# S5 states with real and imaginary part of one group on the 128 partitions, and one row load of the S5 time steps, in a hybrid encoder trunk

## The chip, the cores and the metric

The kernel runs on one core of a Trainium2 chip. The metric is the device time of one execution in microseconds (us). Times stand as the median of several runs. One further execution is taken by the hardware profiler; all rows below come from it.

## The reference

One residual layer over 2048 tokens of width 1024, in float32. The normalised input goes through one projection into twelve 512-wide pieces and a gate. Four branches (S5, retention, differential attention, memory attention) read the pieces; their outputs are gated, projected, merged and put through an output projection. The change touches the S5 branch alone: 32 groups of 16 channels, each with a diagonal complex state of 64 numbers.

```python
def s5_branch(u, lam_re, lam_im, log_dt, b_re, b_im, c_re, c_im, d_skip, w_glu, b_glu):
    ...
    dt = jnp.exp(log_dt.astype(f32))[:, None]
    mag = jnp.exp(lr * dt)
    ab_re = mag * jnp.cos(li * dt)
    ab_im = mag * jnp.sin(li * dt)
    ...
    bu_re = jnp.einsum('bsgh,gph->bsgp', ug, bb_re)
    bu_im = jnp.einsum('bsgh,gph->bsgp', ug, bb_im)
    ...
    _, _, xr, xi = lax.associative_scan(_ssm_combine, (a_re, a_im, bu_re, bu_im), axis=1)
    y = (jnp.einsum('bsgp,ghp->bsgh', xr, c_re.astype(f32))
         - jnp.einsum('bsgp,ghp->bsgh', xi, c_im.astype(f32)))
    y = y.reshape(bsz, seq, BRANCH_W) + d_skip.astype(f32) * u32
    z = jax.nn.gelu(y)
```

## The kernel before, in words

The sequence is worked in two blocks of 1024 tokens. In each block the stages follow one another: retention, differential attention, the other input projections, then memory attention, merge and output. Large matrix products are made of three passes over split operands (a high part and a rest, names ending in h and l): a weight tile `w_r` is loaded by SP (a DMA queue), ScalarE (ACT) rounds it to `w5h`, and VectorE (DVE) or GpSimd (POOL) makes the rest `w5l` (line 443). At the start the tiles of x are loaded (`n_x`, line 557), scaled by a root mean square whose power is taken on POOL (line 138), turned by TensorE (PE, line 574) and split into `xh` and `xl`; then the first product of retention can begin (lines 74 to 76). `w_r` has four buffers, so the fifth weight load waits until the first tile is split.

The order of the work is written as events with due times; a scheduler below the program then sets the order of each engine's instructions. Each engine runs its own list strictly in order.

S5 runs eight steps of time as one: 128 steps of a scan per block. Its matrices are made once, in `setup_s5`, beside the retention of the first block: four passes over four pairs of groups each, which write to a scratch tensor in HBM, `mats_d`, 1280 columns for each of 16 pairs. Each pass makes a table of cosines and sines (`tab`), the input matrices (`gm`, turned and stored as `ev`), the output matrices (`ca`) and a direct term (`tpad`). `tab` and `gm` share one buffer. The time steps `log_dt` come by two DMAs on ACT's queue (line 1593), element by element, with groups 2j on partitions 0 to 63 and groups 2j+1 on 64 to 127, before the first weights are asked for; POOL takes their exponential (`dt`, line 194).

The scan itself is done beside the input projections of each block: `s5_scan`, once for each of 16 pairs, in steps between the products of the projections (line 1332). Both groups of a pair stand on the partitions, 64 states each, and the free dimension holds real part and imaginary part:

```python
        for g2 in range(2):
            r0 = g2 * 64
            for i in range(2):
                PE.matmul(v[r0:r0 + 64, i * 128:(i + 1) * 128], fm[:, i, r0:r0 + 64], u[:, g2, :], start=True, stop=True)
```

So four products with 64 columns of weights go in. DVE turns the result by the table (lines 998 to 1003), scans (line 1007), turns back (lines 1010 to 1016). For the way out each group takes one product of the direct term and two of the state (real and imaginary), whose weights are zero on the other group's 64 partitions (lines 1021 and 1023); the zeros are stored at setup (line 404). A float32 product of 128 columns shows as two records in the trace.

Of the kernel before, what the change touches and what calls it, by code (L numbers as in the profile page):

```python
# [11 lines left out]
F32 = mybir.dt.float32  # L12
# [3 lines left out]
ALU = mybir.AluOpType  # L16
# [12 lines left out]
NPAIR = 16  # L29
# [7 lines left out]
def bc(ap, pos, n):  # L37
    dims = [list(e) for e in ap.ap]
    dims.insert(pos, [0, n])
    return bass.AP(ap.tensor, ap.offset, dims)  # L40
# [3 lines left out]
def trunk_kernel(ctx, tc, a):  # L44
    nc = tc.nc
    V, A, G, PE, DMA = nc.vector, nc.scalar, nc.gpsimd, nc.tensor, nc.sync
# [10 lines left out]
    const = ctx.enter_context(pool("const"))  # L57
# [56 lines left out]
    rho = const.tile([128, NPAIR], F32, name="rho")  # L114
    ldt = const.tile([128, NPAIR], F32, name="ldt")
    carry = const.tile([128, 2, NPAIR], F32, name="carry")
# [5 lines left out]
    mats_d = dram.tile([128, NPAIR, 1280], F32, name="mats_d")  # L122
# [19 lines left out]
    def setup_vectors(p):  # L142
# [3 lines left out]
        r0 = 0  # L146
        for nm, n in rows:
            src = a[nm]
# [4 lines left out]
        pt = ps_tr()  # L153
# [7 lines left out]
        V.tensor_scalar(HEAD_G, HEAD_G, 0.5 * (1.0 - LAMBDA_INIT), None, op0=ALU.mult)  # L161
        lt = p.tile([128, 4, 64], F32, name="lt")
# [12 lines left out]
    def setup_s5(p):  # L175
# [5 lines left out]
        def tt(o, x, y, op, eng=V):  # L181
            eng.tensor_tensor(o, x, y, op=op)
# [16 lines left out]
        t0, t1 = small("t0"), small("t1")  # L199
# [12 lines left out]
        c1 = 6.28125  # L212
# [53 lines left out]
        tt(rho, t0, t0, ALU.mult)  # L266
# [29 lines left out]
        zero = p.tile([128, 128], F32, name="zero")  # L296
        V.memset(zero, 0.0)
        dsk = p.tile([32, 16], F32, name="dsk")
        DMA.dma_start(out=dsk, in_=a["ssm_d"][0].rearrange("(g h) -> g h", h=16))
        pt = ps_tr()  # L300
# [3 lines left out]
        m = 4  # L304
        for j0 in range(0, n, m):
# [23 lines left out]
            DMA.dma_start(out=mats_d[:, js, 1024:1280], in_=tab.rearrange("p j r c -> p j (r c)"))  # L329
# [27 lines left out]
            for j in range(0, m, 2):  # L357
                pt = ps_tr()
                for q in range(4):
                    PE.transpose(pt[:, q * 128:(q + 1) * 128],  # L360
                                 gm[:, q % 2, j + q // 2].rearrange("p s h -> p (s h)"), ident)
                ev = p.tile([128, 2, 256], F32, name="ev", bufs=1)
                A.copy(ev.rearrange("p a b -> p (a b)"), pt)
                DMA.dma_start(out=mats_d[:, j0 + j:j0 + j + 2, 0:256], in_=ev)
                yield
# [32 lines left out]
            for g2 in range(2):  # L398
                r0, r1 = g2 * 64, 64 - g2 * 64
                for i in range(2):  # L400
                    c0 = 256 + (g2 * 2 + i) * 128
                    DMA.dma_start(out=mats_d[r0:r0 + 64, js, c0:c0 + 128],
                                  in_=ca[r0:r0 + 64, i, :, 1:9, :].rearrange("p j s h -> p j (s h)"))
                    DMA.dma_start(out=mats_d[r1:r1 + 64, js, c0:c0 + 128], in_=bc(zero[r1:r1 + 64], 1, m))
                yield
# [17 lines left out]
            for s in range(8):  # L423
                for g2 in range(2):
                    DMA.dma_start(out=mats_d[s * 16:(s + 1) * 16, js, 768 + g2 * 128:896 + g2 * 128],
                                  in_=tpad[:, :, g2, 128 - 16 * s:256 - 16 * s])
                if s % 4 == 3:
                    yield
# [558 lines left out]
    def s5_scan(b, j, p, u, mt):  # L987
        fm, em0, em1, dm, tb = [mt[:, i, :].rearrange("p (r c) -> p r c", r=2) for i in range(5)]
        v = ps_o()
        for g2 in range(2):  # L990
            r0 = g2 * 64
            for i in range(2):
                PE.matmul(v[r0:r0 + 64, i * 128:(i + 1) * 128], fm[:, i, r0:r0 + 64], u[:, g2, :], start=True, stop=True)
        v2 = v[:, 0:256].rearrange("p (r c) -> p r c", r=2)
        cosb, sinb = bc(tb[:, 0, :], 1, 2), bc(tb[:, 1, :], 1, 2)
        p1 = p.tile([128, 2, 128], F32, name="s_p1", tag="s_p1", bufs=1)
        p2 = p.tile([128, 2, 128], F32, name="s_p2", tag="s_p2", bufs=1)
        V.tensor_tensor(p1, v2, cosb, op=ALU.mult)
        V.tensor_tensor(p2, v2, sinb, op=ALU.mult)
        yield  # L1000
        w = p.tile([128, 2, 128], F32, name="s_w", bufs=1)
        V.tensor_tensor(w[:, 0, :], p1[:, 0, :], p2[:, 1, :], op=ALU.add)
        V.tensor_tensor(w[:, 1, :], p1[:, 1, :], p2[:, 0, :], op=ALU.subtract)
        y = p.tile([128, 2, 128], F32, name="s_y", bufs=1)
        rb = rho[:, j:j + 1].to_broadcast([128, 128])
        for i in range(2):
            V.tensor_tensor_scan(y[:, i, :], rb, w[:, i, :], carry[:, i, j:j + 1], op0=ALU.mult, op1=ALU.add)
        q1 = p.tile([128, 2, 128], F32, name="s_q1", tag="s_p1", bufs=1)
        q2 = p.tile([128, 2, 128], F32, name="s_q2", tag="s_p2", bufs=1)
        V.tensor_tensor(q1, y, cosb, op=ALU.mult)  # L1010
        V.tensor_tensor(q2, y, sinb, op=ALU.mult)
# [3 lines left out]
        V.tensor_tensor(x[:, 0, 1:129], q1[:, 0, :], q2[:, 1, :], op=ALU.subtract)  # L1015
        V.tensor_tensor(x[:, 1, 1:129], q2[:, 0, :], q1[:, 1, :], op=ALU.add)
        V.tensor_copy(carry[:, :, j], x[:, :, 128])
        yield
        for g2 in range(2):
            out = v[:, 256 + g2 * 128:384 + g2 * 128]  # L1020
            PE.matmul(out, dm[:, g2, :], u[:, g2, :], start=True, stop=False)
            for i in range(2):
                PE.matmul(out, (em0, em1)[g2][:, i, :], x[:, i, 0:128], start=False, stop=i == 1)
# [555 lines left out]
    for b in range(NBLK):  # L1579
# [4 lines left out]
        if b == 0:  # L1584
            with ExitStack() as sx:
# [5 lines left out]
                for g2 in range(2):  # L1591
                    src = a["ssm_log_dt"]
                    A.dma_start(out=ldt[g2 * 64:(g2 + 1) * 64, :],
                                in_=bass.AP(src.tensor, src.offset + g2, [[0, 64], [2, NPAIR]]))
# [107 lines left out]
```

## Time and profile before

| what | value |
|---|---|
| three runs, median (lowest to highest) | 3048.71 us (3043.44 to 3057.92) |
| the profiled execution, its own time | 3045.78 us |
| its span, first to last instruction | 3043.5 us |
| PE busy | 2899.1 us, 95% |
| PE weight loads busy | 2381.9 us, 78% |
| DVE / ACT / POOL busy | 1920.5 / 1332.3 / 1247.0 us |
| mean granted TensorE clock | 0.990 |
| DMA, mean over the span | 116 GB/s |

A row of the view by windows gives, for a stretch of the span, its length, then the busy time and the count of instructions of PE, of PE's weight loads, of DVE, ACT and POOL, then the granted clock, the DMA engines' busy share and GB/s. A row of the timeline gives start, duration, engine, line, operation, tiles and count; in brackets stands how long the engine sat idle before it, and what ended that. SPq and ACTq are DMA issues.

### The profile page before, as it was taken

To read this page: it belongs to the slowest core of one execution; us is meant where nothing else is said; L and a number is where in the kernel's file an instruction comes from. 1 tells how busy PE (TensorE), PEld (TensorE's weight loads), DVE (VectorE), ACT (ScalarE), POOL (GpSimd) and SP (SyncE) were. 2 spreads that over 40 slices of the span, in tenths; PEclk is the share of its full clock that TensorE was granted. 3 is DMA by queue.
4 is the path that set the end of the run, shared out by engine and by line. 5 is a ranking of instruction groups with operands and counts; after the bars stand their busy time and mean duration, and the time that the engine had idled before them with its cause. 6 is when DMAs were issued, how large, how long until landed. Compare 5 with 4: busy or idle time off the path is not lost. (4 is left out here: it accounts for less than half of the span.)

```text
span 3043.5 us, 43500 instructions
## 1 busy us (share of the span) xinstructions
PE 2899.1 (95%) x14514; PEld 2381.9 (78%) x14514; DVE 1920.5 (63%) x4613; ACT 1332.3 (44%) x3357; POOL 1247.0 (41%) x1157
## 2 busy tenths in 40 slices
PE   5999999998999999999999999999999999999999
PEld 4777877777888888777788878878878888887777
DVE  5885587766655545656544378888766555446654
ACT  3323355563333344423433257767733333444332
POOL 2543533334444442555132242232244444434560
PEclk9999999999999999999999999999999999999999
DMA  5332422233444436555521220120134444355653
GB/s 154 97 92 77 126 68 68 68 97 119 141 150 142 134 109 204 188 182 175 161 69 43 63 66 22 58 61 21 59 115 142 144 142 137 125 184 166 194 167 96
DMA packets 319341, 351.75 MB, mean 116 GB/s; under 512 B 28479, under 2 KB 238478, under 8 KB 319118
## 3 DMA queue, kind: packets, MB, share of 16 engines
q1 hardware_dynamic: 314734, 340.59, 35.7%
q0 software_dynamic: 2304, 8.39, 0.9%
q8 instruction: 114, 1.87, 0.3%
q14 instruction: 109, 0.89, 0.1%
q10 hardware_dynamic: 2080, 0.01, 0.0%
HBM read 247.98 MB, written 100.93 MB: 115 GB/s over the span
## 5 line engine op out<-in xcount | busy, mean ns | idle before, releaser
L1294 POOL TENSOR_TENSOR p_l<-p_r,p_h 128x512 fp32r<-128x512 f32 x260 | 368.4, 1420 | 458.3 <-ACT p_h L1293 445.3
L74 PE MATMUL mm<-w5h,xh 128*128 128x512 f32 x1024 | 436.3, 426 | 17.9 <-ACT xh L577 16.5
L75 PE MATMUL mm<-w5l,xh 128*128 128x512 f32 x1024 | 406.7, 397 | 3.5 <-POOL w5l L443 3.5
L76 PE MATMUL mm<-w5h,xl 128*128 128x512 f32 x1024 | 406.9, 397 | 0.0
L138 POOL TENSOR_TENSOR rms_r<-rms_m,mhalf 128x1 f32<-128x1 f32 (+1 forms) x228 | 179.0, 787 | 488.2 <-DVE rms_m L136 422.6
L1293 ACT CAST p_h<-p_r 128x512 fp32r<-128x512 f32 x260 | 160.3, 621 | 376.6 <-PE mm L1332 85.8
L758 ACT ACTIVATE pr<-sc,nm 128x512 f32<-128x512 f32 (+3 forms) x320 | 200.1, 626 | 148.0 <-DVE nm L756 146.4
L74 PEld LDWEIGHTS mm<-w5h,xh 128*128 128x128 f32 x1024 | 195.2, 191 | 48.3 <-ACT xh L577 16.9
L76 PEld LDWEIGHTS mm<-w5h,xl 128*128 128x128 f32 x1024 | 194.2, 190 | 43.9
L75 PEld LDWEIGHTS mm<-w5l,xh 128*128 128x128 f32 x1024 | 195.8, 191 | 32.1 <-POOL w5l L443 4.7
L75 PE MATMUL sc<-br_l,w1h 128*128 128x512 f32 x496 | 197.3, 398 | 6.9 <-DVE br_l L1212 6.9
L74 PE MATMUL sc<-br_h,w1h 128*128 128x512 f32 x496 | 200.5, 404 | 3.3 <-DVE mg_g L1265 3.3
L756 DVE TENSOR_REDUCE nm<-sc 128x1 f32<-128x512 f32 (+3 forms) x320 | 193.2, 604 | 9.3 <-PE sc L752 5.1
L76 PE MATMUL sc<-br_h,w1l 128*128 128x512 f32 x496 | 197.3, 398 | 0.0
L1266 POOL TENSOR_TENSOR mg<-mg,mg_g 128x512 f32<-128x512 f32 x96 | 140.9, 1471 | 91.9 <-DVE mg_g L1265 83.8
L806 PEld LDWEIGHTS o<-vt,at 128*128 128x128 f32 x1088 | 142.4, 193 | 38.0 <-ACT at L799 29.6
L806 PE MATMUL o<-vt,at 128*128 128x128 f32 x1088 | 152.0, 279 | 16.6 <-ACT at L799 16.5
L460 POOL TENSOR_TENSOR w1l<-w_r,w1h 128x512 fp32r<-128x512 f32 x86 | 119.4, 1401 | 113.3 <-ACT w1h L459 95.8
L443 POOL TENSOR_TENSOR w5l<-w_r,w5h 128x512 fp32r<-128x512 f32 x72 | 96.0, 1336 | 109.9 <-ACT w5h L442 73.7
L1332 PE MATMUL mm<-xh,p_h 128*128 128x512 f32 x336 | 134.0, 399 | 0.3 <-ACT p_t L1402 0.3
L1332 PE MATMUL sc<-xl,p_h 128*128 128x512 f32 x336 | 131.6, 392 | 2.7 <-DVE xl L1367 2.7
L1332 PE MATMUL sc<-xh,p_h 128*128 128x512 f32 x336 | 131.3, 391 | 0.6 <-ACT p_h L1293 0.6
(396 smaller groups left out, 7653.6 us busy)
## 6 DMA issues: line engine op xcount, KB each, us to landing
p_r<-in_w_in SPq DMA_DIRECT2D x88, 512.0 KB
w_r<-in_w_in SPq DMA_DIRECT2D x144, 256.0 KB
me_d<-p_t SPq DMA_DIRECT2D x128, 256.0 KB
mg_g<-me_d SPq DMA_DIRECT2D x64, 512.0 KB
s_m<-mats_d SPq DMA_DIRECT2D x32, 640.0 KB
w_r<-in_w_branch SPq DMA_DIRECT2D x64, 256.0 KB
w_r<-br SPq DMA_DIRECT2D x64, 256.0 KB
n_x<-in_x SPq DMA_DIRECT2D x16, 512.0 KB
```

Source lines behind the costliest of these rows:

```text
L74: PE.matmul(out, l[0], r[0], start=first, stop=False)
L75: PE.matmul(out, l[0], r[1], start=False, stop=False)
L76: PE.matmul(out, l[1], r[0], start=False, stop=last)
L138: G.tensor_tensor(r, m, mhalf[:, 0:n], op=ALU.pow)
L460: G.tensor_tensor(lo, raw, hi.bitcast(F32), op=ALU.subtract)
L756: V.tensor_reduce(nm, s[:, 0:n], axis=AX.X, op=ALU.max, negate=True)
L758: A.activation(e[:, 0:n], s[:, 0:n], AF.Exp, bias=nm, accum_out=self.zz[:, m, c:c + 1])
L806: PE.matmul(self.o[:, 0:128], self.at[c][:, q * 128:(q + 1) * 128], self.st["vts"][c][:, q, :], start=c == 0 and q == 0, stop=c * 4 + q == ...
L1266: G.tensor_tensor(dst, dst, t, op=ALU.add)
L1293: A.copy(hi, x)
L1294: G.tensor_tensor(lo, x, hi.bitcast(F32), op=ALU.subtract)
L1332: PE.matmul(o, l[:, k, :], r, start=first and k == 0 and q == 0, stop=k == 3 and q == 2, skip_group_check=True)
```

## The change

The state is laid out anew: the partitions hold the real part (0 to 63) and the imaginary part (64 to 127) of one group, and the free dimension holds the two groups of a pair. One product with 128 columns of weights brings a group in, one takes it out. A turn by the table then needs the other half of the partitions, which two DVE instructions on 64 partitions each read crosswise (`turned`). The table in `mats_d` is stored for both halves, with a negated sine for one, in eight stores in place of one for each pass; `ca` takes four stores in place of eight; `rho` is copied to the new layout; `ev` is put in order by two ACT copies in place of one. The time steps are loaded on SP as one row, repeated for all partitions, inside `setup_vectors`, and two DVE copies pick the groups out of it.

```diff
+        row = p.tile([128, NPAIR, 2], F32, name="ldt_r")
+        DMA.dma_start(out=row.rearrange("p j g -> p (j g)"), in_=a["ssm_log_dt"][0].partition_broadcast(128))
+        for g2 in range(2):
+            V.tensor_copy(ldt[g2 * 64:(g2 + 1) * 64, :], row[g2 * 64:(g2 + 1) * 64, :, g2])
...
-        tt(rho, t0, t0, ALU.mult)
+        tt(t1, t0, t0, ALU.mult)
+        for i in range(2):
+            for g2 in range(2):
+                V.tensor_copy(rho[i * 64:(i + 1) * 64, g2, :], t1[g2 * 64:(g2 + 1) * 64, :])
...
-            DMA.dma_start(out=mats_d[:, js, 1024:1280], in_=tab.rearrange("p j r c -> p j (r c)"))
+            neg = big[1][:, 0:m * 128].rearrange("p (j c) -> p j c", j=m)
+            ts(neg, tab[:, :, 1, :], -1.0, ALU.mult)
+            for i in range(2):
+                for g2 in range(2):
+                    r0, c0 = g2 * 64, 768 + g2 * 128
+                    for c1, src in ((c0, tab[:, :, 0, :]), (c0 + 256, (neg, tab[:, :, 1, :])[i])):
+                        DMA.dma_start(out=mats_d[i * 64:(i + 1) * 64, js, c1:c1 + 128], in_=src[r0:r0 + 64])
...
-                    DMA.dma_start(out=mats_d[r1:r1 + 64, js, c0:c0 + 128], in_=bc(zero[r1:r1 + 64], 1, m))
...
     def s5_scan(b, j, p, u, mt):
-        fm, em0, em1, dm, tb = [mt[:, i, :].rearrange("p (r c) -> p r c", r=2) for i in range(5)]
+        fm, em, dm, cos, sin = [mt[:, i, :].rearrange("p (r c) -> p r c", r=2) for i in range(5)]
         v = ps_o()
         for g2 in range(2):
-            r0 = g2 * 64
-            for i in range(2):
-                PE.matmul(v[r0:r0 + 64, i * 128:(i + 1) * 128], fm[:, i, r0:r0 + 64], u[:, g2, :], start=True, stop=True)
+            PE.matmul(v[:, g2 * 128:(g2 + 1) * 128], fm[:, g2, :], u[:, g2, :], start=True, stop=True)
...
+        def turned(out, x):
+
+            V.tensor_tensor(out[0:64], x[64:128], sin[64:128], op=ALU.mult)
+            V.tensor_tensor(out[64:128], x[0:64], sin[0:64], op=ALU.mult)
+
...
-        V.tensor_tensor(p2, v2, sinb, op=ALU.mult)
+        turned(p2, v2)
...
-        V.tensor_tensor(q2, y, sinb, op=ALU.mult)
+        turned(q2, y)
...
-            for i in range(2):
-                PE.matmul(out, (em0, em1)[g2][:, i, :], x[:, i, 0:128], start=False, stop=i == 1)
+            PE.matmul(out, em[:, g2, :], x[:, g2, 0:128], start=False, stop=True)
...
-                for g2 in range(2):
-                    src = a["ssm_log_dt"]
-                    A.dma_start(out=ldt[g2 * 64:(g2 + 1) * 64, :],
-                                in_=bass.AP(src.tensor, src.offset + g2, [[0, 64], [2, NPAIR]]))
```

The scheduler's order moves with it at three places. The first is POOL's list at the start, from its first root mean square on; `dt` is the exponential of the time steps, `rqk` belongs to retention. Before:

```order
L138 TENSOR_TENSOR rms_r<-rms_m,mhalf 128x1 [waits DVE_49]
L194 TENSOR_TENSOR dt<-ebase,ldt 128x16 [waits DMAHW2_49,DMAHW0_49]
L443 TENSOR_TENSOR w5l<-w_r,w5h 128x512 [waits DMAHW5_49,Activation_49]
L138 TENSOR_TENSOR rms_r<-rms_m,mhalf 128x1 [waits DVE_49]
L443 TENSOR_TENSOR w5l<-w_r,w5h 128x512 [waits DMAHW7_49,Activation_49]
```

and now:

```order
L138 TENSOR_TENSOR rms_r<-rms_m,mhalf 128x1 [waits DVE_49]
L454 TENSOR_TENSOR w5l<-w_r,w5h 128x512 [waits DMAHW3_49,Activation_49]
L138 TENSOR_TENSOR rms_r<-rms_m,mhalf 128x1 [waits DVE_49]
L454 TENSOR_TENSOR w5l<-w_r,w5h 128x512 [waits DMAHW5_49,Activation_49]
...
L908 TENSOR_TENSOR rqk<-ram,rbm 128x256 [waits DVE_49]
L198 TENSOR_TENSOR dt<-ebase,ldt 128x16 [waits DVE_49]
L206 TENSOR_TENSOR mag<-ebase,t_865 128x16 [waits DVE_49]
```

`dt` has moved from the second place behind the power of the first tile to the eleventh, and waits for DVE's copies in place of a DMA.

The second is SP's list at the second pass of `setup_s5`, where the table is stored (`big_1616` holds the negated sine, `bi` is the next pass's input matrix). Before:

```order
L425 DMA mats_d<-tpad 16x4x128 [waits DMAHW2_49]
L329 DMA mats_d<-tab 128x4x256 [waits DMAHW3_49,DVE_49,Pool_49]
L335 DMA bi<-in_ssm_b_re 128x4x16 [waits DMAHW4_49,DVE_49]
```

and now:

```order
L436 DMA mats_d<-tpad 16x4x128 [waits DMAHW0_49]
L340 DMA mats_d<-tab 64x4x128 [waits DMAHW1_49,DVE_49]
L340 DMA mats_d<-big_1616 64x4x128 [waits DMAHW2_49,DVE_49]
L340 DMA mats_d<-tab 64x4x128 [waits DMAHW3_49]
L340 DMA mats_d<-big_1616 64x4x128 [waits DMAHW4_49]
L340 DMA mats_d<-tab 64x4x128 [waits DMAHW5_49]
L340 DMA mats_d<-tab 64x4x128 [waits DMAHW6_49,Pool_49]
L340 DMA mats_d<-tab 64x4x128 [waits DMAHW7_49]
L340 DMA mats_d<-tab 64x4x128 [waits DMAHW0_49]
L346 DMA bi<-in_ssm_b_re 128x4x16 [waits DMAHW1_49,DVE_49]
```

One store has become eight, ahead of the next pass's loads.

The third is DVE's list at the same pass; `big` is the scratch of the complex products, and `gm` takes `tab`'s buffer. Before:

```order
L182 TENSOR_TENSOR big_1606<-fi,bi 128x64 [waits DMAHW0_49]
L182 TENSOR_TENSOR tab<-tab,big_1605 128x4x128 [waits DVE_49]
L182 TENSOR_TENSOR big_1605<-fr,bi 128x64 [waits DMAHW7_49,DVE_49,Pool_49]
L182 TENSOR_TENSOR bb<-big_1605,big_1606 128x64 [waits DVE_49]
...
L182 TENSOR_TENSOR gm<-big_1605,big_1606 128x512 [waits DMAHW3_49,DVE_49,Pool_49]
```

and now:

```order
L186 TENSOR_TENSOR tab<-tab,big_1615 128x4x128 [waits DVE_49]
L190 TENSOR_SCALAR big_1616<-tab 128x512 [waits Pool_49]
L186 TENSOR_TENSOR big_1615<-fr,bi 128x64 [waits DMAHW5_49,DVE_49]
...
L186 TENSOR_TENSOR big_1616<-fi,bi 128x64 [waits DMAHW4_49,DMAHW2_49,DVE_49]
L186 TENSOR_TENSOR bb<-big_1615,big_1616 128x64 [waits DVE_49]
...
L186 TENSOR_TENSOR gm<-big_1615,big_1616 128x512 [waits DMAHW3_49,DMAHW5_49,DMAHW1_49,DMAHW6_49,DMAHW0_49,DMAHW7_49,DVE_49,Pool_49]
```

The second product into `big` now waits for the two stores of the negated sine, 13 instructions behind the first, and `gm` waits for the six stores of `tab`.

## Rows read from the trace of the kernel before

**Rows 1.** Windows: the first 40 us, S5's setup, and the projections of both blocks

```profile
0.00:40.00 40.00, 8.46 (x31) 6.68 (x32) 11.69 (x23) 11.17 (x19) 10.89 (x14) 1.00 0.44 135
...
100.00:250.00 150.00, 138.92 (x735) 109.28 (x735) 127.04 (x396) 43.84 (x135) 79.89 (x67) 0.97 0.37 98
...
725.00:1077.00 352.00, 352.00 (x1717) 289.04 (x1716) 202.38 (x394) 134.75 (x234) 159.81 (x118) 1.00 0.43 141
...
2265.00:2616.00 351.00, 350.39 (x1706) 287.30 (x1705) 199.58 (x391) 133.34 (x232) 157.37 (x117) 1.00 0.43 142
```

**Rows 2.** Timeline of the start, all engines

```profile
0.74 1.46 ACTq L1593 DMA_DIRECT2D ldt<-in_ssm_log_dt  x2
...
2.26 19.86 SPq L432 DMA_DIRECT2D w_r<-in_w_in  x4
...
26.15 1.06 ACT L565 ACTIVATE n_junk<-n_x 128x1024 bf16<-128x1024 f32 x1 [20.68 <-DMA n_x<-in_x]
...
26.50 2.91 POOL L194 TENSOR_TENSOR dt<-ebase,ldt 128x16 f32<-128x16 f32 x1 [20.20 <-DMA ldt<-in_ssm_log_dt]
...
29.38 1.27 POOL L443 TENSOR_TENSOR w5l<-w_r,w5h 128x512 fp32r<-128x512 f32 x1
...
30.41 0.79 PE L74 MATMUL mm<-w5h,xh 128*128 128x512 f32 x1 [16.50 <-ACT xh L577]
...
30.67 3.80 SPq L432 DMA_DIRECT2D w_r<-in_w_in  x4
...
41.91 0.40 PE L76 MATMUL mm<-w5h,xl 128*128 128x512 f32 x1
```

**Rows 3.** Windows of the start: while the time steps are under way, and behind them

```profile
10.00:16.00 6.00, 1.97 (x8) 1.57 (x8) 1.28 (x1) 0.00 (x0) 0.00 (x0) 1.00 0.06 3
...
26.00:30.00 4.00, 0.00 (x0) 0.00 (x0) 0.85 (x2) 3.54 (x7) 3.50 (x2) 1.00 0.86 265
```

**Rows 4.** Timeline of PE, one pair of the scan: in, and out

```profile
740.04 0.66 PE L993 MATMUL o<-s_u,s_m 128*64 128x128 f32 x8
740.63 0.51 PE L1332 MATMUL sc<-x_t2h,p_h 128*128 128x512 f32 x1
...
748.97 0.38 PE L1021 MATMUL o<-s_u,s_m 128*128 128x128 f32 x2
...
750.22 0.47 PE L1332 MATMUL mm<-xh,p_h 128*128 128x512 f32 x1
```

**Rows 5.** Instructions on the tile s_m: count, then shortest, median, longest in ns

```profile
L1023 PE MATMUL o<-s_x,s_m x256: 274/275/276, 749.2 to 2608.6; 128*128 128x128 f32 x128
L1021 PE MATMUL o<-s_u,s_m x128: 270/274/276, 749.0 to 2608.1; 128*128 128x128 f32 x128
```

**Rows 6.** Timeline of DVE and POOL in the same pair; last, another line's instructions

```profile
740.76 0.42 DVE L998 TENSOR_TENSOR s_p<-o,s_m 128x256 f32<-128x256 f32 x1 [2.64 <-DMA p_r<-in_w_in]
...
743.86 0.29 DVE L1015 TENSOR_TENSOR s_x<-s_q,s_q 128x128 f32<-128x128 f32 x1
...
744.24 1.29 POOL L1294 TENSOR_TENSOR p_l<-p_r,p_h 128x512 fp32r<-128x512 f32 x1 [2.34 <-ACT p_h L1293]
...
744.67 1.01 DVE L1016 TENSOR_TENSOR s_x<-s_q,s_q 128x128 f32<-128x128 f32 x1
...
L714 DVE TENSOR_TENSOR kt<-tr,kt x16: 692/693/694, 368.0 to 2152.8; 64x512 fp32r<-64x512 f32 x16
```

**Rows 7.** Stores to mats_d: count, then shortest, median, longest issue in ns

```profile
L404 SPq DMA_DIRECT2D mats_d<-zero x16: 605/622/677, 63.4 to 73.5; - x16
L402 SPq DMA_DIRECT2D mats_d<-ca x16: 574/588/627, 128.0 to 250.4; - x16
...
L329 SPq DMA_DIRECT2D mats_d<-tab x4: 366/376/382, 112.4 to 229.5; - x4
```

**Rows 8.** Timeline of the second setup pass: the table's store, and gm

```profile
150.48 0.38 SPq L329 DMA_DIRECT2D mats_d<-tab  x1
...
156.75 0.67 DVE L182 TENSOR_TENSOR gm<-big,big 128x512 f32<-128x512 f32 x1
```

More of the change, by code (lines that the diff above doesn't have):

```diff
@@ L113, in trunk_kernel @@
     lam2 = const.tile([128, 2], F32, name="lam2")
-    rho = const.tile([128, NPAIR], F32, name="rho")
+    rho = const.tile([128, 2, NPAIR], F32, name="rho")
     ldt = const.tile([128, NPAIR], F32, name="ldt")
@@ L295, in setup_s5 @@
         yield
-        zero = p.tile([128, 128], F32, name="zero")
-        V.memset(zero, 0.0)
         dsk = p.tile([32, 16], F32, name="dsk")
@@ L362, in setup_s5 @@
                 ev = p.tile([128, 2, 256], F32, name="ev", bufs=1)
-                A.copy(ev.rearrange("p a b -> p (a b)"), pt)
+                for q in range(2):
+                    A.copy(ev[:, q, :].rearrange("p (g i s) -> p i g s", g=2, i=2),
+                           pt[:, q * 256:(q + 1) * 256].rearrange("p (i g s) -> p i g s", g=2, i=2))
                 DMA.dma_start(out=mats_d[:, j0 + j:j0 + j + 2, 0:256], in_=ev)
@@ L398, in setup_s5 @@
             for g2 in range(2):
-                r0, r1 = g2 * 64, 64 - g2 * 64
+                r0, c0 = g2 * 64, 256 + g2 * 128
                 for i in range(2):
-                    c0 = 256 + (g2 * 2 + i) * 128
-                    DMA.dma_start(out=mats_d[r0:r0 + 64, js, c0:c0 + 128],
+                    DMA.dma_start(out=mats_d[i * 64:(i + 1) * 64, js, c0:c0 + 128],
                                   in_=ca[r0:r0 + 64, i, :, 1:9, :].rearrange("p j s h -> p j (s h)"))
-                    DMA.dma_start(out=mats_d[r1:r1 + 64, js, c0:c0 + 128], in_=bc(zero[r1:r1 + 64], 1, m))
                 yield
@@ L424, in setup_s5 @@
                 for g2 in range(2):
-                    DMA.dma_start(out=mats_d[s * 16:(s + 1) * 16, js, 768 + g2 * 128:896 + g2 * 128],
+                    DMA.dma_start(out=mats_d[s * 16:(s + 1) * 16, js, 512 + g2 * 128:640 + g2 * 128],
                                   in_=tpad[:, :, g2, 128 - 16 * s:256 - 16 * s])
@@ L1014, in s5_scan @@
         V.tensor_copy(x[:, :, 0], carry[:, :, j])
-        V.tensor_tensor(x[:, 0, 1:129], q1[:, 0, :], q2[:, 1, :], op=ALU.subtract)
-        V.tensor_tensor(x[:, 1, 1:129], q2[:, 0, :], q1[:, 1, :], op=ALU.add)
+        V.tensor_tensor(x[:, :, 1:129], q1, q2, op=ALU.subtract)
         V.tensor_copy(carry[:, :, j], x[:, :, 128])
@@ L1021, in s5_scan @@
             PE.matmul(out, dm[:, g2, :], u[:, g2, :], start=True, stop=False)
-            for i in range(2):
-                PE.matmul(out, (em0, em1)[g2][:, i, :], x[:, i, 0:128], start=False, stop=i == 1)
+            PE.matmul(out, em[:, g2, :], x[:, g2, 0:128], start=False, stop=True)
         yv = v[:, 256:512]
```

13 lines of the change are left out of this document (6 added, 7 removed).

## The prediction

> **What bounds the kernel now.** I read the windows by stage first, since the change touches three places far apart in time, and each must be judged by the engine that ends last there. In [rows 1] the first number behind the stretch is PE's busy time. The two projection stages that hold the S5 scan have PE busy 352.00 of 352 us and 350.39 of 351: there every product taken off PE is time saved, while DVE has work for 202.38 us, POOL for 159.81. In the setup stretch (100 to 250 us) PE is busy 138.92 of 150 and DVE 127.04, so both have little air. In the first 40 us PE works 8.46 us.
>
> The timeline says why the start is so empty. ACT's queue asks for the time steps at 0.74 us; POOL's exponential of them ends an idle time of 20.20 us only at 26.50 [rows 2]. POOL is in order, so the first `w5l` behind it starts at 29.38 and the first big product at 30.41. The weight loads suffer too: four issues take SP 19.86 us from 2.26 on, and the second tile of x, asked for before them, lets ACT go on at 26.15 only. From 10 to 16 us the DMA engines move 3 GB/s though loads are queued; at once behind the time steps, from 26 to 30 us, 265 GB/s [rows 3]. So the element-wise load holds up two things, POOL's list and the DMA path of everything asked for later.
>
> **The start.** The load as a row removes both holds. Of 128 partitions each gets one piece, behind the weights on SP, and `dt` moves behind eight POOL instructions that feed the first products. What it is worth: the DMA moved 135 GB/s over 40 us [rows 1], 5.4 MB, by the end of the first tile's product (41.91 us, [rows 2]). At the 265 GB/s of [rows 3] that takes 20.4 us, with about 1.5 us of issue 22, so at most 18 us earlier. From below: were the DMA path slow for another reason, only `dt` itself (2.91 us) would leave the front of POOL's list, 3 us. I take **16**, near the upper end, because 265 GB/s follow in the very window in which the time steps are in; something is kept back because the last four weight loads (issued from 30.67 on) wait for the splits of the first four. PE is the bound behind it, so this shift stays.
>
> **The scan's products.** Per pair, PE now spends 740.04 to 740.63 on the way in, 0.59 us for four products with 64 columns (eight records), and 748.97 to 750.22 on the way out, 1.25 us for six (twelve records) [rows 4]. The count for the way out is 256 and 128 records over 32 pairs [rows 5], eight and four for each. So a record of full width takes 1.25 / 12 = 0.104 us from start to start; its 0.275 us in [rows 5] overlaps the next ones. After the change there are two products in (four records, 0.42) and four out (eight records, 0.83). Saved: 0.17 + 0.42 = 0.59 us a pair, times 32 = **19**. The upper bound is 22, if the gap of about 0.1 us that now stands ahead of the narrow products goes too. For a lower bound let the way in save nothing, 0.42 x 32 = 13.
>
> A rule speaks against the term of the way in. The Trainium skill, TensorEngine Tiling (Array Packing), Performance Considerations, says that weights of at most 64 columns let two such products run side by side on halves of the array; four narrow ones would then cost what two full ones do, and the way in would save nothing. The row shows 0.59 us where the rate of full records would give 0.42 for four and 0.83 for eight, so the narrow ones stand between: partly side by side at best. I go by the row.
>
> **DVE in the scan.** Two half-partition products replace one, twice a pair. Half the partitions are no cheaper: an instruction that reads across the halves, 64 x 512, takes 0.692 us [rows 6], against 0.67 for 128 x 512 [rows 8]. So each half costs the 0.42 of 128 x 256 [rows 6], 0.84 more a pair; one instruction in place of two for the sum and for the difference gives back 0.3 or more. DVE has about 9 us of idle time per pair (150 us in 16 pairs, [rows 1]), which hides it.
>
> **The setup.** The zero stores go (16 issues of 0.62, [rows 7]); they ran ahead of weight loads that wait for buffers anyway, so I count nothing. Stores of `ca` fall from eight to four in a pass, but the table's one store (0.376) becomes eight on 64 partitions, each some 0.588 like those of `ca` [rows 7]: 4.3 us more on SP, four times. They matter through two new waits on DVE: the scratch that now holds the negated sine is free, and `gm` may overwrite `tab`, only after the stores. In the second pass `gm` started 6.3 us behind the issue of the table's store [rows 8], and eight issues alone take 4.7, so `gm` just fits; the product into the scratch, which followed at once before, does not, and the scheduler put 13 instructions ahead of it. Behind these waits in DVE's list stand the retention's `rsm` and `ram`, for which PE waits. Bounds: nothing, or all 4.3 us on PE in all four passes, 17. DVE's extra work is at most 4 x 0.67 for the negations, 2.7 us. Its idle 23 us in that stretch are nearly 6 for a pass, which covers most; I take 1 us a pass, 4. `dt`, 2.91 us of POOL, now stands among the retention's `rqk` and the powers for x, with DVE's copies ahead of it and DVE's product of `dt` behind: between 0 and 3 us, I take 2. The second ACT copy per `ev`, the copies of `rho` and of the time steps are a few tenths each beside PE's work: nothing. Setup together: **+6**, bounds 0 and 23.
>
> **Sum.** -16 - 19 + 6 = -29. Against the profiled execution's 3045.78 us that is 3016.8. The median of the three runs shown lies 2.9 us above that execution, the lowest 2.3 below. I forecast **3018 us**, 1% less than the median.
>
> **Rivals.**
>
> 1. *The start keeps its pace.* If the slow weight loads have another cause than the time steps, only 3 us go there: -3 - 19 + 6 = -16, 3030 us. For it speaks that the time steps are few bytes; against it [rows 2, 3], where the rate jumps as they land. 0.10.
> 2. *The setup takes it back.* The stores come late in all four passes, `gm` and the scratch wait, and PE loses the upper bound of 23: -16 - 19 + 23 = -12, 3034 us. For it: DVE is busy 85% there and in order. Against: the scheduler has moved work into the gap. 0.12.
> 3. *The narrow products already ran side by side.* Four of them, two by two, then take what two full ones do: the way in saves nothing, -16 - 13 + 6 = -23, 3023 us. For it: 0.59 us is less than full records would take; against it: it is more than two full products would. 0.10. The tiling rule above would have it so.
> 4. *Slower: the way out waits for DVE.* Before, the chain from `v` to the last part of `x` ended at 745.68 (744.67 + 1.01, [rows 6]) and PE wanted it at 748.97 [rows 4], 3.3 us of slack a pair. The chain now has two more instructions (0.84), and those with both inputs in SBUF can be held by POOL: line 1016 took 1.01 us where its twin at line 1015 took 0.29, and POOL's split ran from 744.24 to 745.53 [rows 6]. Every microsecond beyond the slack costs 32 us in all. Five such instructions are left; all held as long as line 1016 (0.72 each) make the chain 4.4 longer, 1.1 us too late, +35 - 29 = +6. The kernel gets slower by over 0.5% from some 1.5 us too late on, which needs the five held for 0.8 us on average; held for the whole 1.29, the chain would be 4 us too late, 128 us, 3145 us. Against it: nearly all would have to be held in every pair, and line 1015 was not held at all. The Trainium skill, SBUF — State Buffer, Who interferes with whom, states such a lock between a DVE instruction with two SBUF inputs and a GpSimd one that reads SBUF; lines 1015 and 1016 agree with it. 0.04, of which 0.03 slower.
>
> **How the numbers follow.** The forecast has the other 0.64. About 0.5% (15 us) is what a measurement of this kernel can tell from no change, so faster means below 3033.5. Faster: forecast, rival 3, nearly all of rival 1 and a third of rival 2, 0.64 + 0.10 + 0.09 + 0.02, and I say 0.85. Slower: 0.03. The same: 0.12. The range: the best bounds, -18 - 22 + 0, give 3006, and a run as far under the profiled execution as the lowest of before 3003; upward it takes in rivals 1 and 2, 3036 with the spread.
>
> **What would show it.** In the profile after: no POOL idle time behind the time steps, four weight issues in some 2 us rather than 20, the first big product near 14 us and the first tile's product done near 26. In the projections, PE still fully busy, the way in 0.42 and the way out 0.83 us, each pair 0.6 us shorter. In the setup, DVE idle at the scratch product and `gm` behind the table's stores, PE losing a few microseconds. The forecast is wrong if the first big product still comes after 25 us, if PE shows waits for `x` at the way out, or if PE's idle time between the start and the end of setup grows by more than 15 us.

## The result and the profile after

The changed kernel takes 3017.28 us (median of four runs, 3013.41 to 3024.76), the kernel before 3048.77 beside it. The ratio is 0.9897, with a 95% interval from 0.9871 to 0.9922: faster by 1%. The forecast was 3018. The profiled execution took 3017.78 us, its span is 3016.0 us, 27.5 less than before.

The windows of the changed kernel, with the columns of [rows 1]; the projections are shorter now, so their stretches end earlier:

```profile
0.00:40.00 40.00, 26.31 (x114) 20.88 (x114) 22.72 (x57) 17.25 (x35) 16.75 (x19) 1.00 0.69 212
10.00:16.00 6.00, 1.66 (x5) 0.89 (x5) 5.11 (x5) 4.19 (x8) 3.28 (x3) 1.00 0.81 243
100.00:250.00 150.00, 132.21 (x717) 104.52 (x715) 122.29 (x379) 39.76 (x132) 69.09 (x63) 0.98 0.41 96
725.00:1064.00 339.00, 339.00 (x1592) 284.05 (x1591) 215.52 (x393) 135.66 (x233) 155.11 (x118) 1.00 0.44 146
2252.00:2590.00 338.00, 337.48 (x1580) 282.30 (x1579) 212.20 (x390) 134.60 (x231) 154.24 (x117) 1.00 0.44 147
```

PE does 26.31 us of work in the first 40 where it did 8.46 [rows 1]; from 10 to 16 us the DMA moves 243 GB/s where it moved 3 [rows 3]. In the projections PE is as full as it was. Between 100 and 250 us, in the setup, it is busy 6.7 us less than before: 132.21 us for 717 instructions against 138.92 for 735 [rows 1].

The timeline of the start, all engines, to be laid beside [rows 2]:

```profile
2.13 2.51 SPq L443 DMA_DIRECT2D w_r<-in_w_in  x4
...
8.07 1.06 ACT L576 ACTIVATE n_junk<-n_x 128x1024 bf16<-128x1024 f32 x1 [2.35 <-DMA n_x<-in_x]
...
9.80 1.26 POOL L454 TENSOR_TENSOR w5l<-w_r,w5h 128x512 fp32r<-128x512 f32 x1 [3.25 <-ACT w5h L453]
...
12.71 0.80 PE L74 MATMUL mm<-w5h,xh 128*128 128x512 f32 x1 [2.66 <-ACT xh L588]
...
24.10 0.39 PE L76 MATMUL mm<-w5h,xl 128*128 128x512 f32 x1
...
33.43 2.92 POOL L198 TENSOR_TENSOR dt<-ebase,ldt 128x16 f32<-128x16 f32 x1 [1.52 <-DVE ldt L165]
...
36.64 2.90 POOL L206 TENSOR_TENSOR mag<-ebase,t 128x16 f32<-128x16 f32 x1 [0.29 <-DVE th L186]
```

Four weight issues take 2.51 us in place of 19.86, the second tile of x is there at 8.07 in place of 26.15, and the last of the first tile's 24 products starts at 24.10 in place of 41.91: 17.8 us earlier. `dt` and `mag`, two exponentials on POOL, now stand at 33 to 40 us, amid retention's first units; `dt` stood ahead of the first product before.

PE in one pair of the scan, to be laid beside [rows 4] (the first row is the last product ahead of the pair, the last the next pair's way in):

```profile
739.76 0.40 PE L1343 MATMUL mm<-xh,p_l 128*128 128x512 f32 x1
740.00 0.61 PE L1002 MATMUL o<-s_u,s_m 128*128 128x128 f32 x4
740.36 0.48 PE L1343 MATMUL sc<-x_t2h,p_h 128*128 128x512 f32 x1
...
748.62 0.39 PE L1033 MATMUL o<-s_u,s_m 128*128 128x128 f32 x2
...
749.43 0.48 PE L1343 MATMUL mm<-xh,p_h 128*128 128x512 f32 x1
...
760.41 0.61 PE L1002 MATMUL o<-s_u,s_m 128*128 128x128 f32 x4
```

The way in takes 0.36 us (0.59 before), the way out 0.81 (1.25), and a pair comes every 20.42 us where it came every 21.27: 319.00 us from the first pair's way in to the sixteenth's before, 306.30 now, both in 15 periods.

**Where the time went** is read best from fixed places of the program. Retention of the first block works in 32 units, numbered from 0; each has one gate on ACT (tile `si_t`, line 611 before, 622 after). The table shows by how many us a gate starts earlier than in the kernel before (a minus stands for later), and the first product of the scan (740.04 us before), for the changed kernel and the experiments below:

| kernel | unit 0 | unit 5 | unit 10 | unit 30 | scan | time (us) |
|---|---|---|---|---|---|---|
| changed | 17.8 | 10.8 | 6.0 | 2.6 | 0.0 | 3017.28 |
| row load alone | 18.5 | 15.4 | 16.1 | 17.7 | 17.7 | 3033.73 |
| new state alone | -0.1 | -2.0 | -9.3 | -10.3 | -11.7 | 3027.94 |
| elements early, used late | 1.1 | -2.7 | -8.3 | -12.2 | -16.0 | 3035.72 |
| own buffers | 18.6 | 12.2 | 12.4 | 10.1 | 8.0 | 3007.01 |
| own buffers, second time | 19.0 | 12.5 | 13.1 | 9.2 | 8.4 | 3006.50 |
| row first | 17.3 | 15.5 | 9.8 | 8.5 | 6.9 | 3012.36 |
| row first, own buffers | 16.3 | 14.4 | 13.6 | 10.9 | 9.3 | 3010.69 |
| row behind the weights, own buffers | 18.5 | 17.4 | 18.9 | 15.1 | 11.5 | 3006.34 |
| own buffer for gm alone | 18.4 | 11.8 | 7.4 | -6.0 | -8.8 | 3023.46 |
| two stores | 18.9 | 12.4 | 12.5 | 9.3 | 8.4 | 3005.69 |
| narrow way in | 19.3 | 12.8 | 7.8 | 3.4 | -0.2 | 3030.30 |

So the changed kernel wins 17.8 us at the start and has lost all of it before the scan begins: 7 by unit 5, 8 more in the four setup passes (units 5 to 30), the rest up to the scan. What is left in the end comes from the scan: 12.7 us in each block and about 2 behind it. Each row of the table is one profiled execution. Two pairs of rows show how far to trust it: own buffers, run twice, differ by up to 0.9 us, and the kernel with the narrow way in, whose setup is the changed one, differs from the changed kernel by up to 2.0.

### The profile page after: what moved, and what is told of

Same layout as the page of the kernel before. It is cut to its first block, busy times and chain, and to the rows that moved or that the text cites. A ratio compares the mean times of both kernels' runs of the same rounds, so it can differ in the third digit from the quotient of the medians.

```text
span 3016.0 us, 43039 instructions
## 1 busy us (share of the span) xinstructions
PE 2872.6 (95%) x14258; PEld 2372.2 (79%) x14258; DVE 1958.8 (65%) x4622; ACT 1336.7 (44%) x3365; POOL 1234.1 (41%) x1157
## 5 line engine op out<-in xcount | busy, mean ns | idle before, releaser
L1305 POOL TENSOR_TENSOR p_l<-p_r,p_h 128x512 fp32r<-128x512 f32 x260 | 359.8, 1387 | 439.9 <-ACT p_h L1304 436.9
L817 PE MATMUL o<-vt,at 128*128 128x128 f32 x1088 | 150.9, 278 | 17.2 <-ACT at L810 17.1
```

The source lines that it names most:

```text
L817: PE.matmul(self.o[:, 0:128], self.at[c][:, q * 128:(q + 1) * 128], self.st["vts"][c][:, q, :], start=c == 0 and q == 0, stop=c * 4 + q == ...
L1305: G.tensor_tensor(lo, x, hi.bitcast(F32), op=ALU.subtract)
```

## Experiments

Four questions were put: is the gain of the start lost to what setup got, or would any earlier start be lost; which hold at the start mattered; what takes the setup's time; and why a pair gives 0.85 us instead of 0.59.

### The row load alone

The kernel before, with the row load and its two copies (as in the change) in place of the two element-wise loads.

> The kernel before, with the row load of the time steps as the only edit. In the changed kernel retention's unit 0 ran 17.8 us earlier than before, unit 3 13.2, unit 25 2.8, and the first product of the scan 0.04: the gain of the start was all gone. Theory A (the new stores and waits of the setup took it): here the setup is the old one, so the 13 us that are left behind dt's new place stay, unit 25 still runs about 13 us earlier, and the kernel takes about 3036 us. Theory B (S5's setup, with DVE busy 85% and in order, ends when it ends, and takes back any earlier start): unit 25 runs some 3 us earlier or less, and the kernel takes 3045 to 3049 us. Between: about 3041.

Measured: 3033.73 us (six runs, 3025.39 to 3040.00; the profiled one is the lowest), ratio 0.9946 [0.9927, 0.9964]. It is 18.5 us ahead at unit 0 and still 17.7 ahead at the scan. The gain of the start lasts through an unchanged setup; what the changed kernel loses there, the new setup takes.

### The new state alone

The changed kernel with the element-wise load as before:

```diff
-        row = p.tile([128, NPAIR, 2], F32, name="ldt_r")
...
+                    A.dma_start(out=ldt[g2 * 64:(g2 + 1) * 64, :],
+                                in_=bass.AP(src.tensor, src.offset + g2, [[0, 64], [2, NPAIR]]))
```

> The changed kernel with the element-wise load of the time steps back at its old place. Both theories: first product at about 30.4 us, 20.42 us from pair to pair of the scan, 27 us saved there. Theory A: the new stores and waits cost their 8 to 15 us here too, unit 25 runs 8 or more us later than before, about 3032 us. Theory B: nothing is lost, unit 25 runs within 2 us of before, about 3022 us.

Measured: 3027.94 us (four runs), ratio 0.9934 [0.9917, 0.9952]. It comes to the scan 11.7 us late and ends 18.2 us ahead by its span. With the row load the price is larger: 17.7 us won by the row alone less 11.7 would leave 6, and the changed kernel has none.

### Elements loaded early, used late

The element-wise load stands in its old place, but into a tile of its own, copied to `ldt` inside `setup_vectors` (by adding a tile of zeros, `nil`); so POOL's list no longer waits for it.

```diff
+        V.tensor_tensor(ldt, ldt_e, nil, op=ALU.add)
...
+                    A.dma_start(out=ldt_e[g2 * 64:(g2 + 1) * 64, :],
```

> The changed kernel with the element-wise load at its old place, into a tile of its own, and DVE taking it over at the place where it now takes the row: the DMA path is burdened as before, POOL's list is free of the wait. If the burdened DMA path sets the start: four weight issues take some 20 us again and the first product comes near 28 us. If POOL's wait sets it: the first product comes at 13 to 16 us.

Measured: 3035.72 us (one run). The timeline of its start:

```profile
2.26 19.66 SPq L443 DMA_DIRECT2D w_r<-in_w_in  x4
...
26.02 1.06 ACT L576 ACTIVATE n_junk<-n_x 128x1024 bf16<-128x1024 f32 x1 [20.35 <-DMA n_x<-in_x]
...
27.75 1.27 POOL L454 TENSOR_TENSOR w5l<-w_r,w5h 128x512 fp32r<-128x512 f32 x1 [21.25 <-ACT w5h L453]
```

POOL has nothing of the time steps in front, and nothing is earlier: the issues take 19.66 us, x lands at 26, and unit 0 gains 1.1 us. So of the two holds it is the DMA path, held by the elements, that set the start. The Trainium skill, DMA: Bandwidth & Descriptors, Rules for kernel authors, asks to join many small transfers into one; the row load does that, and the 17.8 us agree. One DMA queue (q10), which the changed kernel does not use, has 2080 packets in the kernel before; with the row load in the elements' place, further below, it has 144.

### Buffers of its own for gm and the negated sine

`gm` gets its own buffer instead of `tab`'s, and the negated sine stands in `gm`'s second half instead of in the scratch `big`; so neither product waits for the table's stores.

```diff
-            neg = big[1][:, 0:m * 128].rearrange("p (j c) -> p j c", j=m)
+            gm = p.tile([128, 2, m, 8, 16], F32, name="gm")
+            neg = gm[:, 1].rearrange("p j s h -> p j (s h)")
...
-            gm = p.tile([128, 2, m, 8, 16], F32, name="gm", tag="tab")
```

> The changed kernel with gm in a buffer of its own, and the negated sine in gm's second half in place of the scratch; the eight stores stay. Theory A, by its waits: scratch and first half of gm no longer wait, the passes lose 5 to 10 us less, unit 25 runs 8 to 12 us earlier than before, 3008 to 3012 us. Theory A, by the stores' issue time alone, or theory B: within 2 us of the changed kernel, 3017.

Measured: 3007.01 us (four runs), ratio 0.9863 [0.9846, 0.9880], and once more beside a later experiment:

> The kernel with buffers of its own for gm and the negated sine once more, beside the one before it: 3007 us, 10 us less than the changed kernel, and 2 to 5 above the kernel with the row behind the first weights if that theory holds.

3006.50 us (four runs), 0.9859 [0.9842, 0.9875]. This beats both kernels, by 10 us the changed one. DVE's list at the second pass shows how; first the changed kernel, from the negated sine to the first part of `gm`:

```profile
143.99 0.43 DVE L190 TENSOR_SCALAR big<-tab 128x512 f32<-128x512 f32 x1 [1.19 <-POOL tab L186]
...
158.05 0.68 DVE L186 TENSOR_TENSOR gm<-big,big 128x512 f32<-128x512 f32 x1
```

then the kernel with its own buffers:

```profile
138.02 0.43 DVE L190 TENSOR_SCALAR gm<-tab 128x512 f32<-128x512 f32 x1 [1.18 <-POOL tab L186]
...
141.30 0.69 DVE L186 TENSOR_TENSOR gm<-big,big 128x512 f32<-128x512 f32 x1
```

14.1 us in the one, 3.3 in the other. In the four passes it is 9.0, 14.1, 8.0 and 12.1 against 3.5, 3.3, 3.3 and 3.7. As a wait the trace shows little of it, since the scheduler filled the gap with later work; two rows of the changed kernel's first pass show what is left:

```profile
106.92 0.23 DVE L186 TENSOR_TENSOR big<-fi,bi 128x64 f32<-128x64 f32 x1 [2.15 <-DMA mats_d<-big]
```

and, on PE, which turns `gm`:

```profile
111.68 0.33 PE L371 MATMUL tr<-ident,gm 128*128 128x128 f32 x1 [2.49 <-DVE rms_m L136]
```

What this costs shows on PE. From the gate of unit 0 to that of unit 30 the profile has the same 1296 PE instructions in each of these kernels; first the kernel before, then the changed one, then own buffers:

```profile
43.72:303.14 259.42, 242.20 (x1296) 194.55 (x1295) 199.71 (x684) 86.73 (x255) 113.46 (x108) 0.98 0.37 100
25.91:300.50 274.59, 243.41 (x1296) 194.87 (x1295) 208.65 (x694) 87.27 (x263) 111.05 (x109) 0.97 0.37 94
25.07:293.08 268.01, 243.86 (x1296) 197.03 (x1295) 206.63 (x694) 86.70 (x264) 113.46 (x109) 0.97 0.38 96
```

For this work PE is busy within 2 us as long in all three. It sits idle 17.2, 31.2 and 24.2 us. So the new setup costs 14.0 us of idle PE time, and own buffers give back half of that. The edit also moves the order of DVE's list; what part of the half is owed to the order and not to the waits was not separated.

Behind such a gap the clock falls too. The windows of the changed kernel around that place:

```profile
108.00:110.00 2.00, 1.19 (x7) 0.82 (x5) 2.00 (x6) 0.14 (x1) 1.37 (x2) 1.00 0.05 6
110.00:112.00 2.00, 0.32 (x2) 0.33 (x3) 2.00 (x5) 0.37 (x2) 0.57 (x2) 1.00 0.39 60
112.00:114.00 2.00, 0.47 (x3) 0.03 (x1) 1.01 (x3) 0.16 (x1) 1.81 (x2) 0.92 0.00 0
114.00:116.00 2.00, 1.92 (x9) 1.74 (x9) 0.23 (x2) 0.89 (x3) 0.00 (x0) 0.50 0.00 0
116.00:118.00 2.00, 2.00 (x12) 1.53 (x11) 0.54 (x3) 0.00 (x0) 0.00 (x0) 0.50 0.39 131
118.00:120.00 2.00, 2.00 (x6) 1.41 (x6) 1.92 (x6) 0.00 (x0) 1.73 (x1) 0.50 0.15 33
120.00:122.00 2.00, 2.00 (x13) 1.79 (x12) 0.80 (x2) 1.27 (x5) 1.89 (x2) 0.88 0.00 0
```

PE is busy 1.98 of 6 us while it waits for `gm`; behind that the granted clock is 0.50, the 1.2 GHz level, for three windows, and full again by 122. Summed over the seven windows the clock that was not granted is (0.08 + 3 x 0.50 + 0.12) x 2 = 3.4 us, nearly as much as the 4.0 us of idle time ahead of it. The Trainium skill, TensorE: Matmul & The Clock Gate, Part 1: The HAM clock gate, says that idle time costs PE its fast clock for a while; these rows agree. But this is not what own buffers give back: they keep 1.00 throughout this first pass and lose it elsewhere, and from unit 0 to unit 30 the granted clock is 0.97 in both.

### Own buffer for gm alone

Only the second half of that edit: `gm` has its own buffer, the negated sine stays in the scratch.

> The changed kernel with a buffer of its own for gm alone: gm no longer waits for the six stores of the table, while the product into the scratch still waits for the two stores of the negated sine. Theory A (gm's wait costs the more, since it stands behind eight issues): most of the 7.4 us that both buffers gave comes back, unit 30's gate some 8 us earlier than in the kernel before, against 2.6 in the changed kernel. Theory B (the wait of the scratch product, the only one that the trace names, 2.15 us, costs the more): unit 30 stays near 3 to 5 us.

Measured: 3023.46 us (one run), 16 us more than with both buffers. It is also 6 us above the changed kernel's median though a wait was taken away, but within that kernel's runs (3013.41 to 3024.76). From the negated sine to `gm` it takes 9.0 us in the first pass and 12.5 in the second, hardly less than the 9.0 and 14.1 of the changed kernel: the wait that counts is that of the scratch product, and `gm` comes behind it anyway. Theory B was right on that, but not on unit 30, which is 6.0 us behind the kernel before and 8.6 behind the changed one. From unit 0 to unit 30, as above:

```profile
25.35:309.18 283.83, 253.75 (x1296) 202.11 (x1295) 209.88 (x694) 86.63 (x263) 111.09 (x109) 0.93 0.36 91
```

PE sits idle 30.1 us, no longer than in the changed kernel, but is busy 253.75 us with the same instructions, 10.3 more, at a granted clock of 0.93 in place of 0.97. Here the loss is the clock's. The windows between units 14 and 18:

```profile
155.00:158.00 3.00, 1.16 (x4) 1.07 (x5) 3.00 (x6) 0.88 (x3) 2.37 (x2) 0.80 0.52 142
158.00:161.00 3.00, 3.00 (x13) 2.47 (x13) 2.56 (x6) 0.91 (x2) 1.98 (x3) 0.63 0.42 123
...
167.00:170.00 3.00, 1.44 (x6) 0.59 (x5) 3.00 (x5) 0.00 (x0) 2.90 (x2) 1.00 0.56 134
170.00:173.00 3.00, 2.73 (x18) 2.00 (x19) 2.24 (x11) 0.77 (x3) 1.03 (x1) 0.58 0.45 94
173.00:176.00 3.00, 3.00 (x16) 1.91 (x13) 2.13 (x9) 0.00 (x0) 0.00 (x0) 0.50 0.31 97
176.00:179.00 3.00, 3.00 (x10) 2.42 (x9) 1.84 (x12) 0.00 (x0) 0.00 (x0) 0.50 0.23 41
```

Twice PE starves for about half of a window while DVE is full, and twice the clock drops behind it. The edit moved the order of DVE's list, and so the places of the gaps; why the clock falls more often behind these was not tried. So a single wait cannot be priced by its length here.

### Two stores in place of eight

Own buffers, and the table stored by two DMAs of 128 partitions; it leaves out the sine's sign and the layout, so the scan turns by another table.

```diff
+            for c0 in (768, 1024):
+                DMA.dma_start(out=mats_d[:, js, c0:c0 + 256], in_=tab.rearrange("p j r c -> p j (r c)"))
```

> The kernel with buffers of its own for gm and the negated sine, and in place of the table's eight stores two of 128 partitions, which fill the same columns with the table as it stands, so the turns of the scan go by a wrong table. It leaves out six issues of some 0.6 us on SP in each pass, and the sine's sign. Theory A (with the waits gone the issues themselves are hidden): unit 30's gate stays near 10 us earlier than in the kernel before, and the time near 3007. Theory B (the issues hold up the loads and stores behind them): unit 30 goes toward 14 us, and the time toward 3003.

Measured: 3005.69 us (one run), and 9.3 us ahead at unit 30, as with eight stores. The issues are hidden once nobody waits for them, though in the changed kernel each takes what was put down for it:

```profile
L340 SPq DMA_DIRECT2D mats_d<-tab x24: 575/621/807, 100.9 to 234.0; - x24
L340 SPq DMA_DIRECT2D mats_d<-big x8: 575/598/622, 103.7 to 231.3; - x8
```

### The row first

The changed kernel, with the row load first on ACT's queue, where the elements stood, and `dt` early on POOL.

```diff
+                A.dma_start(out=row.rearrange("p j g -> p (j g)"), in_=a["ssm_log_dt"][0].partition_broadcast(128))
```

> The changed kernel with the row load put where the element-wise load stood before, first on ACT's queue, with DVE's two copies right behind it, so that POOL takes dt near the front of its list again. Theory (dt and mag, 2.9 us each on POOL at 33 to 40 us, hold the powers and the chain behind them, and so cost 4 to 7 us in retention's units 2 to 5): the first big product still starts near 12.7 us, unit 5's gate is some 15 us earlier than in the kernel before rather than 10.8, and about 4 us of it last to the end, 3011 to 3015 us. Rival (the units 2 to 5 lose their time to something else, the last weight loads or DVE's list): unit 5 stays near 11 us earlier and the time at 3017. Second rival (the passes' waits absorb what is won ahead of them): unit 5 near 15, unit 25 still near 3, the time at 3017.

Measured: 3012.36 us (five runs), ratio 0.9884 [0.9864, 0.9905]. Unit 5 is 15.5 us ahead in place of 10.8: most of the time lost in units 2 to 5 goes with the late `dt`. `mag` has hardly moved (35.35 us, 36.64 in the changed kernel), so this gain does not come from it, though the expectation named both. Nor does a late `dt` cost this much by itself: in the row load alone it comes at 32.69 us, and that kernel loses 3.1 us by unit 5 and 0.8 by the scan. It costs more beside the new setup, and why was not tried. The median is 4.9 us lower, but the runs scatter over the changed kernel's (3005.86 to 3018.68, the profiled one the lowest) and the intervals of the two ratios overlap, so a gain in time is not shown.

### Both repairs, in two ways

Own buffers with the row first:

> Both repairs together: the input matrices gm and the negated sine in a buffer of their own, and the row load first on ACT's queue with dt near the front of POOL's list. Theory (the two losses, units 2 to 5 and the passes, are separate): unit 5's gate about 15 us earlier than before, unit 30's about 14 and the first product of the scan about 12, against 10 and 8 with the buffers alone; 3001 to 3004 us. Rival (the passes absorb what comes earlier, whoever brings it): 3007 us, as with the buffers alone.

Measured: 3010.69 us (four runs), ratio 0.9873 [0.9854, 0.9892]: no better than own buffers. In front of the weights the row costs the start (x lands at 6.40 us, not 4.56, four weight issues take 5.09 us, not 2.51), and unit 0 is 16.3 ahead instead of 18.6 to 19.0. That is not what the time shows, though. At the scan this kernel leads own buffers, second time, by 0.9 us, and the last pair of the second block begins at 2560.19 us in the one, at 2560.18 in the other. Behind that it takes 448.9 us to the end against 443.6: the same 1941 PE instructions keep PE busy 427.65 us against 423.46, at a clock of 0.98 against 0.99. What lowers the clock there was not tried. To mend the start, the row went behind the first four weight loads, on SP:

> The kernel with buffers of its own for gm and the negated sine, and the row load on SP right behind the first four weight loads, its copies behind; dt then stands fifth in POOL's list from the first power on, where POOL sat idle for 3.09 us. Theory (the row in front of the weights cost 2 us of start, dt in the middle of the powers 2 to 5 us of units 2 to 5; in this place it costs neither): unit 0's gate some 18.5 us earlier than before, unit 5's 15 or more, unit 30's 12 to 14, 3002 to 3005 us. Rival (the passes absorb it): unit 30's near 10, 3007 us. From below: dt holds back the third and fourth rest of the weights, unit 0's gate near 16, 3009 us.

`dt` then falls into a gap that POOL had there:

```profile
15.28 2.91 POOL L194 TENSOR_TENSOR dt<-ebase,ldt 128x16 f32<-128x16 f32 x1 [2.03 <-DVE ldt L1603]
```

Unit 5 is 17.4 us ahead, unit 30 15.1, the scan 11.5: the theory held for all of these. But the time is 3006.34 us (four runs), 0.9858 [0.9844, 0.9873], the same as with own buffers alone. The 3.1 us by which it leads at the scan are gone when the second block's scan begins (2254.02 against 2253.88 us). From the last pair of the first scan to the first pair of the second, of this kernel and of own buffers, second time:

```profile
1034.88:2254.02 1219.14, 1173.68 (x6045) 973.39 (x6044) 791.88 (x1892) 604.47 (x1624) 454.32 (x454) 0.99 0.32 100
1037.97:2253.88 1215.91, 1173.38 (x6046) 973.14 (x6045) 792.18 (x1892) 604.12 (x1624) 454.42 (x454) 0.99 0.32 100
```

PE is busy as long in both, at the same clock; it sits idle 45.5 us in the one and 42.5 in the other. What it waits for there was not tried and stays open.

### The narrow way in

The changed kernel, but with the way in as four products of 64 columns in the new layout:

```diff
-            PE.matmul(v[:, g2 * 128:(g2 + 1) * 128], fm[:, g2, :], u[:, g2, :], start=True, stop=True)
+            for i in range(2):
+                PE.matmul(v[i * 64:(i + 1) * 64, g2 * 128:(g2 + 1) * 128], fm[:, g2, i * 64:(i + 1) * 64], u[:, g2, :], start=True, stop=True)
```

> The changed kernel with the way in of the scan issued as four products with 64 columns of weights again, in the new layout; the way out stays as changed. Theory A (a change between narrow and full products costs PE time of its own, ahead of and behind them, beside the records): the way in goes back from 0.36 to about 0.59, the gap ahead from 0.24 to about 0.32, something about 0.1 us more behind, the pair's period from 20.42 to 20.8 us, 32 pairs some 13 us, 3030 us. Theory B (only the records count; the rest of the 0.85 us a pair came from the way out): the period goes to 20.65, 7 us in all, 3025 us. Theory C (narrow ones run side by side and cost what full ones do): period 20.42, 3017 us.

Measured: 3030.30 us (one run), span 3028.5, 12.5 more than the changed kernel. PE in its first pair, and the second pair's way in:

```profile
739.87 0.39 PE L1344 MATMUL mm<-xh,p_l 128*128 128x512 f32 x1
740.19 0.66 PE L1003 MATMUL o<-s_u,s_m 128*64 128x128 f32 x8
740.77 0.50 PE L1344 MATMUL sc<-x_t2h,p_h 128*128 128x512 f32 x1
...
742.06 0.39 PE L1344 MATMUL sc<-x_t2h,p_l 128*128 128x512 f32 x1
...
760.99 0.66 PE L1003 MATMUL o<-s_u,s_m 128*64 128x128 f32 x8
```

The period is 20.80 us, 0.38 more than the changed kernel's 20.42, and 32 x 0.38 = 12 is nearly the whole difference. The records themselves account for 0.58 - 0.36 = 0.22. The rest lies around them: the last product ahead takes 0.32 us to the first narrow one, against 0.24 to a full one, and from the first product behind to the sixth it is 1.29 us (740.77 to 742.06) against 1.23 (740.36 to 741.59 in the changed kernel). That is theory A by its period, with less of it behind than was put down.

## Why the prediction was right or wrong

The time was right: 3018 forecast, 3017.28 measured, by the side that was given 0.85. That is in part luck: two terms were off in opposite directions, the setup by 12 us and the scan by 8.

- **The start** (-16). Mechanism right, size nearly: 17.8 us at the first tile's product, just under the 18 that the prediction worked out from the DMA's rate. The slow weight issues and the late x came from the elements, as argued; that POOL's wait mattered too was not borne out, it would have hidden behind x. Every sign named for it is in the rows above, the first big product at 12.71 rather than 14. What was wrong is the sentence that this shift stays: it stays with the setup of before, and not with the new one.
- **The scan's products** (-19, upper bound 22). This term was mis-sized: 0.85 us a pair, not 0.59, so 27 in all, beyond its upper bound. The way out gave what was counted, 0.44. The way in gave 0.38 to 0.39 by the narrow way in, not 0.17. Of that the records themselves are 0.22; the forecast had 0.17 of it, since it priced the new records by the way out's 0.104 us, and four take 0.36. The gap ahead it left to the upper bound (0.1 us; it is 0.08), and the slower products behind it did not see. Rival 3, that narrow products run side by side, falls with the narrow way in: four of them cost 0.38 us more than two full ones. The Trainium skill, TensorEngine Tiling (Array Packing), Performance Considerations, gives weights of at most 64 columns a twofold tiling; these float32 products, issued in this way, do not agree.
- **DVE in the scan.** Hidden, as said. The rows of the changed kernel show each half-partition product at the price of a whole one, and one of them held longer:

```profile
740.64 0.42 DVE L1012 TENSOR_TENSOR s_p<-o,s_m 128x256 f32<-128x256 f32 x1 [2.48 <-DMA p_r<-in_w_in]
741.08 0.43 DVE L1007 TENSOR_TENSOR s_p<-o,s_m 64x256 f32<-64x256 f32 x1
...
744.94 0.68 DVE L1008 TENSOR_TENSOR s_q<-s_y,s_m 64x256 f32<-64x256 f32 x1
...
746.26 0.42 DVE L1028 TENSOR_TENSOR s_x<-s_q,s_q 128x256 f32<-128x256 f32 x1
...
747.20 1.25 DVE L1029 COPY carry<-s_x 128x2 f32<-128x2 f32 x1
```

  x is done at 746.68 and the way out begins at 748.62, so 1.9 us of the 3.3 of slack are left. Rival 4 did not come: the long holds of [rows 6] did not repeat on five instructions. One came behind x, where no term looked: the copy of the carry (line 1029) takes 1.25 us in the median where it took 0.15 before, here beside a split on POOL from 747.14 to 748.43. PE does not wait for it.
- **The setup** (+6, bounds 0 to 23). This is the step that failed. Up to the scan the setup and what stands beside it cost all 17.8 us, inside the bounds and at rival 2's end of them. Two of its terms were too small. For the passes' waits, 1 us each was taken because DVE's idle time and the moved instructions seemed to cover the waits; own buffers give back 8.4 us at the scan and 10.8 in the median, so 2 to 3 us a pass. The cover was real, the trace names hardly a wait on the stores, but the work behind it came 5 to 11 us later, and PE ran dry: 14.0 us more idle time from unit 0 to unit 30, just under the 15 that the prediction named as a sign of being wrong. And `dt` with DVE's chain behind it, taken at 2, cost 5.9 us at unit 30 (15.1 against 9.2 with own buffers); putting it early does not reach the time, since all of it is lost again later. What else of the 17.8 us the new setup takes, beside these two, is not shown.
- **Rivals 1 and 2.** The start did not keep its pace. Rival 2's mechanism happened in great part; its price was hidden by the scan, which gave 8 us more than counted: -17.8 + 17.8 - 27.5.

## What to carry to other kernels

A buffer that is stored to memory and then reused ties the next step to the store; when one store becomes eight, give the stored data a buffer of its own before counting on the scheduler to fill the gap, because moved work is late work. Between two fixed places with the same PE instructions, compare PE's idle time and its busy time each by itself: the one shows waits, the other a fallen clock. And follow a gain at the start along fixed places of the program: a right total can hide that nearly all of it was given back within 300 us.

## What the runs showed that was not expected

- Two element-wise loads held four weight issues for 19.66 us, and the tile of x asked for before them until 26 us, with nobody waiting for the elements themselves; a row load of the same time steps in front of them cost 2 us.
- Narrow float32 products cost time beyond their records, 0.08 us ahead and some 0.06 behind, when they stand between full ones.
- Taking one of two waits away brought unit 30 8.6 us later (one profiled execution): PE was idle no longer, but the granted clock from unit 0 on was 0.93 in place of 0.97, and the same instructions kept PE busy 10.3 us longer.
- 3 us won before the first scan were gone by the second, as 3.0 us more of idle PE time between them at the same clock.
